# Loading the last residual pair in two column halves, and queueing the stores after the first of them

## The chip, the cores and the metric

The kernel runs on one core of a Trainium2 chip. The metric is the time of one execution in microseconds (us), taken on the device. The profile is one further execution with the hardware profiler; its span runs from the first to the last instruction and is 1.8 us shorter than the time (121.2 us for 123.01 in the profiled run of the kernel before).

## The reference

A 3 x 3 convolution with padding 1 over 16 images of 64 channels and 64 x 64 pixels, 64 channels out, plus a residual:

```python
for b in range(batch):
    for co in range(c_out):
        for ci in range(c_in):
            for kh in range(k):
                for kw in range(k):
                    output[b, co] += weight[co, ci, kh, kw] * x_pad[b, ci, kh:kh+h, kw:kw+w]
return (output + residual).astype(np.float32)
```

Input, residual and output are float32, 16.8 MB each. So 50.48 MB (with the weights) have to move, whatever the kernel does.

## The kernel before

Two images form a pair, on 128 partitions. The residual is loaded into one large tile `ro`, the adds write their result into the same tile, and the stores read it. All loads but one, and all stores, are issued by the sync engine, in one queue. I call each of the 16 DMA engines' part of a queue its ring. It is worked off in order of issue: the store issued at 58.71 us lands at 91.1 us, after the load issued just before it, which lands at 81.3 us.

```python
EARLY = (slice(0, 2), slice(2, 4), slice(4, 6), slice(6, 7))
RES = (slice(0, 1), slice(1, 2), slice(2, 4), slice(4, 6), slice(6, 8))
...
def load_ro(i, e):
    if i >= 2:
        e.wait_ge(s_r[i % 2], 16 * (i // 2))
    return e.dma_start(out=ro[:, RES[i], :], in_=res_bc[:, RES[i], :]).then_inc(s_r[i % 2], 16)
...
for p in range(NPAIR):                      # the sync queue: all loads ...
    if p >= NXR:
        nc.sync.wait_ge(s_half, 2 * (p - NXR) + 3)
    ...
        load_x(p)
    if p in (1, 3, 5, 7):
        load_ro((p + 1) // 2, nc.sync)
for pairs in EARLY:                         # ... and then the stores
    nc.sync.wait_ge(s_add, 2 * pairs.stop + 1)
    store(pairs).then_inc(s_out, 16)
```

The last pair is stored in two column halves at the very end. The scalar engine casts and packs the input, the tensor engine convolves, the vector engine adds the residual (32 adds).

Of the kernel before, what the change touches and what calls it, by code (L numbers as in the profile page):

```python
# [15 lines left out]
def kernel(  # L16
# [7 lines left out]
    nc = tc.nc  # L24
# [6 lines left out]
    NPIX = H * W  # L31
    NPAIR = B // 2
# [4 lines left out]
    NXP = 4  # L37
    NZERO = 4 + 2 * NXP
    EARLY = (slice(0, 2), slice(2, 4), slice(4, 6), slice(6, 7))
    RES = (slice(0, 1), slice(1, 2), slice(2, 4), slice(4, 6), slice(6, 8))  # L40

    res_bc = residual.rearrange("(p b) c h w -> (b c) p (h w)", b=2)
    out_bc = out.rearrange("(p b) c h w -> (b c) p (h w)", b=2)
# [7 lines left out]
    ro = pool.tile([128, NPAIR, NPIX], FP32)  # L51
# [7 lines left out]
    sem = lambda name: tc.alloc_semaphore(name)  # L59
    s_w = sem("s_w")  # L60
    s_x = [sem(f"s_x{i}") for i in range(NXR)]
    s_r = [sem(f"s_r{i}") for i in range(2)]
    s_out = sem("s_out")
    s_id = sem("s_id")
    s_half = sem("s_half")
# [5 lines left out]
    def load_x(p):  # L71
        return nc.sync.dma_start(out=xr[p % NXR][:, :], in_=x_bc[128 * p : 128 * p + 128, :]).then_inc(s_x[p % NXR], 16)

    def load_ro(i, e):
        if i >= 2:
            e.wait_ge(s_r[i % 2], 16 * (i // 2))
        return e.dma_start(out=ro[:, RES[i], :], in_=res_bc[:, RES[i], :]).then_inc(s_r[i % 2], 16)

    def store(pairs, cols=slice(0, NPIX)):
        return nc.sync.dma_start(out=out_bc[:, pairs, cols], in_=ro[:, pairs, cols])  # L80
# [21 lines left out]
    def to_the_front(dma):  # L102



        def fixed(ap):
            t = ap.bass_ap.tensor.name
            return mybir.PhysicalAccessPattern(
                ap=ap.ap, offset=ap.bass_ap.offset, dtype=ap.dtype, memref=t, memsetref=t + "_set", bass_ap=ap.bass_ap
            )  # L110

        front = nc.main_func.blocks[0].instructions
        here = nc.cur_bb.bb.instructions
        ins = here.pop()
        assert ins.name == dma.ins.name
        at = next(
            i for i, e in enumerate(front) if e.engine == ins.engine and isinstance(e, mybir.InstDrain)
        )
        front.insert(at, copy.replace(ins, ins=[fixed(a) for a in ins.ins], outs=[fixed(a) for a in ins.outs]))
# [5 lines left out]
    def weight_block(h, half, d, par, kh):  # L125

        at = 64 * half + 32 * h
        return dict(out=wl[at : at + 32, d, :, par, :], in_=tp[0:32, kh, 0:384].rearrange("p (kw co h) -> p kw co h", kw=3, h=2)[:, :, :, h])

    with tc.tile_critical(no_gpsimd_drain=True):  # L130

        for p in range(NPAIR):
            if p >= NXR:

                nc.sync.wait_ge(s_half, 2 * (p - NXR) + 3)
            if p == 0:
                to_the_front(load_x(p))
                nc.sync.dma_start(out=wraw[:, :], in_=w_rows[:, :]).then_inc(s_w, 16)
            else:
                load_x(p)  # L140
            if p in (1, 3, 5, 7):
                load_ro((p + 1) // 2, nc.sync)
        for pairs in EARLY:
            nc.sync.wait_ge(s_add, 2 * pairs.stop + 1)
            store(pairs).then_inc(s_out, 16)


        nc.gpsimd.memset(ident[:, :], 0.0).then_inc(s_id, 1)  # L148
        nc.gpsimd.wait_ge(s_id, 1)
        nc.gpsimd.affine_select(  # L150
            out=ident[:, :],
            in_=ident[:, :],
            compare_op=mybir.AluOpType.not_equal,
            fill=1.0,
            base=0,
            pattern=[[-1, 128]],
            channel_multiplier=1,
        ).then_inc(s_id, 1)
        nc.gpsimd.wait_ge(s_id, 2)
        for t in xp:  # L160
            nc.gpsimd.memset(t[0:64, 0, :], 0.0).then_inc(s_id, 1)  # L161
            nc.gpsimd.memset(t[64:128, J, :], 0.0).then_inc(s_id, 1)  # L162
        nc.gpsimd.memset(wl[0:64, 0, :, 1, :], 0.0).then_inc(s_id, 1)  # L163
        nc.gpsimd.memset(wl[64:128, 1, :, 0, :], 0.0).then_inc(s_id, 1)  # L164


        to_the_front(load_ro(0, nc.scalar))
        for n in range(B):
            p, im = divmod(n, 2)
            hp = slice(64 * im, 64 * im + 64)  # L170
            x4 = xr[p % NXR].rearrange("q (j two w) -> q j two w", two=2, w=W)
            t = xp[n % NXP]
            if im == 0:
                nc.scalar.wait_ge(s_x[p % NXR], 16 * (p // NXR + 1))
            i = nc.scalar.copy(out=t[64:128, 0:J, :], in_=x4[hp, :, 0, :])  # L175
            i.then_inc(s_half, 1)
            if n >= NXP:
                i._wait_ge(s_conv, n - NXP + 1)
            nc.scalar.copy(out=t[0:64, 1 : J + 1, :], in_=x4[hp, :, 1, :]).then_inc(s_pack, 1)  # L179
            if n == 0:  # L180
                nc.scalar.wait_ge(s_id, NZERO + 1)
                for b in blocks[4:]:
                    for h in range(2):
                        i = nc.scalar.copy(**weight_block(h, *b))  # L184
                i.then_inc(s_id, 1)


        nc.vector.wait_ge(s_id, NZERO + 1)
        for k, b in enumerate(blocks[:4]):
            for h in range(2):  # L190
                i = nc.vector.tensor_copy(**weight_block(h, *b))  # L191
                if k == h == 0:
                    i.then_inc(s_bank, 2)
        i.then_inc(s_id, 1)
        for n in range(B):
            p, im = divmod(n, 2)
            hp = slice(64 * im, 64 * im + 64)
            o4 = ro[:, p, :].rearrange("q (j two w) -> q j two w", two=2, w=W)
            psj = ps[n % 2].rearrange("q c j w -> q (c j) w")
            if im == 0:  # L200
                i = next(i for i, pairs in enumerate(RES) if p < pairs.stop)
                nc.vector.wait_ge(s_r[i % 2], 16 * (i // 2 + 1))
            for par in range(2):
                i = nc.vector.tensor_tensor(  # L204
                    out=o4[hp, :, par, :], in0=psj[64 * par : 64 * par + 64, :, :], in1=o4[hp, :, par, :], op=ADD
                )
                if par == 0:
                    i._wait_ge(s_conv, n + 1)

                i.then_inc(s_add if par == 0 or n == B - 1 else s_bank, 1)  # L210


        nc.tensor.wait_ge(s_id, NZERO)
        nc.tensor.wait_ge(s_w, 16)
        wraw3 = wraw.rearrange("p (ci t) -> p ci t", t=9)
        for t in range(9):
            i = nc.tensor.transpose(  # L217
                out=tp[0:32, t // 3, 128 * (t % 3) : 128 * (t % 3) + 128], in_=wraw3[:, :, t], identity=ident[:, :]
            )
        i.then_inc(s_id, 1)  # L220
        nc.tensor.wait_ge(s_id, NZERO + 3)
        with nc.Fori(0, B // NXP, 1, engines=[PE]):
            for n in range(NXP):
                nc.tensor.wait_ge(s_bank, 1).then_inc(s_bank, -1)
                nc.tensor.wait_ge(s_pack, 1).then_inc(s_pack, -1)  # L225
                order = [(1, 0), (1, 1), (0, 0), (0, 1), (2, 0), (2, 1)]
                for i, (kw, d) in enumerate(order):
                    xlo, xhi = max(0, 1 - kw), min(W, W + 1 - kw)
                    for c in range(NCHUNK):
                        j0 = JC * c  # L230
                        m = matmul(
                            ps[n % 2][:, c, :, xlo:xhi],
                            wl[:, d, kw, :, :].rearrange("q r c -> q (r c)"),
                            xp[n][:, j0 + d : j0 + d + JC, xlo + kw - 1 : xhi + kw - 1],
                            i == 0,
                            i == len(order) - 1,
                            c == 0,
                        )
                m.then_inc(s_conv, 1)


    for h in range(2):
        store(slice(NPAIR - 1, NPAIR), slice(NPIX // 2 * h, NPIX // 2 * (h + 1)))
    with tc.tile_critical(sync_engine=mybir.EngineType.Pool, no_gpsimd_drain=True):
        nc.gpsimd.wait_ge(s_out, 16 * len(EARLY))
        tc.free_semaphores([s_w, *s_x, *s_r, s_out, s_id, s_half, s_pack, s_bank, s_conv, s_add])
# [30 lines left out]
```

## Time and profile before

| | before |
|---|---|
| time, median | 122.92 us (122.90 to 122.94) |
| span of the profile | 121.2 us |
| bytes moved, mean rate over the span | 50.48 MB, 416 GB/s |
| rate in a full stretch | 433 GB/s |
| tensor / vector / scalar engine busy | 86.5 / 76.0 / 63.1 us |
| landing of the last load, of the last store | 81.3 us, 120.3 us |

How to read it: the rate in the full stretches against the mean says that the transfers are the bound, and the difference to the span says how little there is to win. The prediction shows the lines.

Besides the page I use the trace's records of single DMA packets: one row of a transfer, its start, duration and size. In steady traffic a packet of 16 KB takes 611 ns and one of 8 KB takes 309 ns, in nearly every record to the nanosecond; the usual one of 12 KB takes 460 ns, of 4 KB 159 ns. I call **the loss** of a stretch the sum of what its packets took beyond that, divided by 16 engines; gaps in which an engine has no packet are counted apart.

### The profile page before, as it was taken

The numbers are of one execution on the slowest core, as the hardware profiler recorded it, in microseconds if no ns is written. First come the engines' busy times: TensorE is split into PE (matmuls) and PEld (weight loads), VectorE is DVE, ScalarE is ACT, GpSimd is POOL, SyncE is SP. The second block draws the span as 40 slices with busy tenths as digits, with TensorE's granted clock in tenths as the row PEclk, the third lists the DMA queues.
The fourth block names the chain that finished last, engine by engine and source line by source line (L and its number), as shares of the span: only waits on it lengthen the run. The fifth ranks groups of instructions, "written<-read, shape, count | busy, mean of one in ns | idle before, by whom it ended". The sixth has DMA issues, their size and how long they took to land.

```text
span 121.2 us, 735 instructions
## 1 busy us (share of the span) xinstructions
PE 86.5 (71%) x393; PEld 10.6 (9%) x105; DVE 76.0 (63%) x40; ACT 63.1 (52%) x37; POOL 2.4 (2%) x16
## 2 busy tenths in 40 slices
PE   0000609999999999999999999999999998000000
PEld 0000300010101010101010101010101010000000
DVE  0000180088989889898988989889898988930000
ACT  4001999999999755995785958659200000000000
POOL 5200000000000000000000000000000000000000
PEclk9999999999999999999999999999999999955555
DMA  7999999999999999999999999999999999999994
GB/s 232 416 427 438 433 433 433 427 433 433 433 427 433 427 433 433 433 433 433 433 433 433 433 422 427 384 378 433 433 427 427 433 427 433 433 427 433 416 430 181
DMA packets 3648, 50.48 MB, mean 416 GB/s; under 512 B 320, under 2 KB 448, under 8 KB 448
## 3 DMA queue, kind: packets, MB, share of 16 engines
q1 hardware_dynamic: 3504, 48.38, 94.3%
q10 hardware_dynamic: 144, 2.10, 4.1%
HBM read 33.70 MB, written 16.78 MB: 416 GB/s over the span
## 4 chain that ended last, share of the span: by engine, by line
PE 70%; DVEq 2%; DVE 2%; issue 0%
PE ps L87 52%; PE ps L86 18%; DVEq L130 2%; DVE ro L204 2%
## 5 line engine op out<-in xcount | busy, mean ns | idle before, releaser
L204 DVE TENSOR_TENSOR ro<-ps,ro 64x2048 f32<-64x2048 f32 x32 | 73.2, 2289 | 16.3 <-PE ps L87 15.8
L87 PE MATMUL ps<-xp,wl 128*128 128x504 bf16 (+1 forms) x288 | 78.9, 383 | 0.0
L175 ACT CAST xp<-xr 64x2048 bf16<-64x2048 f32 x16 | 30.3, 1896 | 21.1 <-DMA xr<-in_x_dram 11.7
L86 PE MATMUL ps<-xp,wl 128*128 128x504 bf16 (+1 forms) x96 | 36.9, 384 | 3.4 <-PEq L225 3.4
L179 ACT CAST xp<-xr 64x2048 bf16<-64x2048 f32 x16 | 30.4, 1897 | 0.4
L86 PEld LDWEIGHTS ps<-xp,wl 128*128 128x128 bf16 x96 | 9.4, 98 | 77.8 <-issue 77.8
L191 DVE CAST wl<-ps 32x192 bf16<-32x192 f32 x8 | 2.8, 348 | 14.9 <-PE ps L217 14.8
L217 PE MATMUL ps<-ident,wraw 128*32 128x128 f32 x9 | 2.1, 413 | 12.6 <-DMA wraw<-in_weight_dram 12.6
L217 PEld LDWEIGHTS ps<-ident,wraw 128*32 128x32 f32 x9 | 1.2, 137 | 13.1 <-issue 12.6
L175 ACT ACT_TABLE_LOAD x1 | 1.3, 1283 | 1.1 <-SPq L130 1.1
L184 ACT CAST wl<-ps 32x192 bf16<-32x192 f32 x4 | 1.2, 306 | 0.0
L162 POOL MEMSET xp<- 64x64 bf16 x4 | 0.6, 147 | 0.2
L161 POOL MEMSET xp<- 64x64 bf16 x4 | 0.6, 145 | 0.2
L150 POOL TENSOR_SCALAR_AFFINE_SELECT ident<-ident 128x128 f32<-128x128 f32 x1 | 0.3, 295 | 0.2 <-POOL ident L148 0.2
L164 POOL MEMSET wl<- 64x192 bf16 x1 | 0.3, 253 | 0.1
L163 POOL MEMSET wl<- 64x192 bf16 x1 | 0.3, 252 | 0.1
L148 POOL MEMSET ident<- 128x128 f32 x1 | 0.2, 205 | 0.7 <-SPq L130 0.7
L261 POOL MEMSET const-bfloat16-1.0<- 128x1 bf16 x1 | 0.1, 112 | 0.0
L261 POOL MEMSET const-uint8-127<- 128x1 uint8 x1 | 0.1, 112 | 0.0
L261 POOL MEMSET const-float32-1.0<- 128x1 f32 x1 | 0.1, 109 | 0.0
L261 POOL MEMSET const-float32-0.0<- 128x1 f32 x1 | 0.1, 104 | 0.2 <-issue 0.2
## 6 DMA issues: line engine op xcount, KB each, us to landing
xr<-in_x_dram SPq DMA_DIRECT2D x8, 2048.0 KB, 14.8
ro<-in_residual_dram SPq DMA_DIRECT2D x3, 4096.0 KB, 23.1
out_dram<-ro SPq DMA_DIRECT2D x3, 4096.0 KB, 32.2
ro<-in_residual_dram ACTq DMA_DIRECT2D x1, 2048.0 KB, 12.1
ro<-in_residual_dram SPq DMA_DIRECT2D x1, 2048.0 KB, 20.2
out_dram<-ro SPq DMA_DIRECT2D x1, 2048.0 KB, 15.7
out_dram<-ro SPq DMA_DIRECT2D x2, 1024.0 KB, 11.4
wraw<-in_weight_dram SPq DMA_DIRECT2D x1, 144.0 KB, 11.4
```

Source lines behind the costliest of these rows:

```text
L86: return e.matmul(out=out_, lhsT=lhsT, rhs=rhs, start=start, stop=stop, skip_group_check=True)
L87: return e.add_instruction(mybir.InstMatmult(name=nc.get_next_instruction_name(), engine=PE, ins=[e.lower_ap(rhs), e.lower_ap(lhsT)], outs ...
L130: with tc.tile_critical(no_gpsimd_drain=True):
L161: nc.gpsimd.memset(t[0:64, 0, :], 0.0).then_inc(s_id, 1)
L162: nc.gpsimd.memset(t[64:128, J, :], 0.0).then_inc(s_id, 1)
L175: i = nc.scalar.copy(out=t[64:128, 0:J, :], in_=x4[hp, :, 0, :])
L179: nc.scalar.copy(out=t[0:64, 1 : J + 1, :], in_=x4[hp, :, 1, :]).then_inc(s_pack, 1)
L184: i = nc.scalar.copy(**weight_block(h, *b))
L191: i = nc.vector.tensor_copy(**weight_block(h, *b))
L204: i = nc.vector.tensor_tensor(out=o4[hp, :, par, :], in0=psj[64 * par : 64 * par + 64, :, :], in1=o4[hp, :, par, :], op=ADD)
L217: i = nc.tensor.transpose(out=tp[0:32, t // 3, 128 * (t % 3) : 128 * (t % 3) + 128], in_=wraw3[:, :, t], identity=ident[:, :])
L261: nc = _bacc.Bacc("TRN2", target_bir_lowering=False, num_devices=1)
```

## The change

Its intent: stores that queue up behind the last loads are to be kept out of the rings until the loads are nearly through, and yet to come early enough that the rings don't run dry. So the last residual load is cut, and its last megabyte covers the time that issuing the stores takes.

```diff
-    RES = (slice(0, 1), slice(1, 2), slice(2, 4), slice(4, 6), slice(6, 8))
+    WHOLE, LEFT, RIGHT = slice(0, NPIX), slice(0, NPIX // 2), slice(NPIX // 2, NPIX)
+    RES = (
+        (slice(0, 1), WHOLE, None),
+        (slice(1, 2), WHOLE, 1),
+        (slice(2, 4), WHOLE, 3),
+        (slice(4, 6), WHOLE, 5),
+        (slice(6, 7), WHOLE, 7),
+        (slice(7, 8), LEFT, 7),
+        (slice(7, 8), RIGHT, 7),
+    )
+    NR = 3
...
-    s_r = [sem(f"s_r{i}") for i in range(2)]
+    s_r = [sem(f"s_r{i}") for i in range(NR)]
...
-            if p in (1, 3, 5, 7):
-                load_ro((p + 1) // 2, nc.sync)
+            for i, (_, _, behind) in enumerate(RES):
+                if behind == p:
+                    load_ro(i, nc.sync)
+
+        wait_ro(nc.sync, len(RES) - 2)
         for pairs in EARLY:
             nc.sync.wait_ge(s_add, 2 * pairs.stop + 1)
             store(pairs).then_inc(s_out, 16)
```

The vector engine waits for every load that holds a part of its pair, and `load_ro` waits modulo three (cut here).

More of the change, by code (lines that the diff above doesn't have):

```diff
@@ L74, in load_ro, with wait_ro @@
     def load_ro(i, e):
-        if i >= 2:
-            e.wait_ge(s_r[i % 2], 16 * (i // 2))
-        return e.dma_start(out=ro[:, RES[i], :], in_=res_bc[:, RES[i], :]).then_inc(s_r[i % 2], 16)
+        pairs, cols, _ = RES[i]
+        if i >= NR:
+            e.wait_ge(s_r[i % NR], 16 * (i // NR))
+        return e.dma_start(out=ro[:, pairs, cols], in_=res_bc[:, pairs, cols]).then_inc(s_r[i % NR], 16)
+    def wait_ro(e, i):
+        e.wait_ge(s_r[i % NR], 16 * (i // NR + 1))
     def store(pairs, cols=slice(0, NPIX)):
@@ L200 @@
             if im == 0:
-                i = next(i for i, pairs in enumerate(RES) if p < pairs.stop)
-                nc.vector.wait_ge(s_r[i % 2], 16 * (i // 2 + 1))
+                for i, (pairs, cols, _) in enumerate(RES):
+                    if pairs.start <= p < pairs.stop:
+                        wait_ro(nc.vector, i)
             for par in range(2):
@@ L239 @@
                 m.then_inc(s_conv, 1)
-    for h in range(2):
-        store(slice(NPAIR - 1, NPAIR), slice(NPIX // 2 * h, NPIX // 2 * (h + 1)))
+    for cols in (LEFT, RIGHT):
+        store(slice(NPAIR - 1, NPAIR), cols)
     with tc.tile_critical(sync_engine=mybir.EngineType.Pool, no_gpsimd_drain=True):
```

## The prediction

> **What bounds the kernel now.** I read the page first, in the order slices, queues, chain; then the table by stretches of the span; then the sync queue's own waits and its timeline. The slices of the page, the traffic line and the chain come first.
>
> ```profile
> DMA  7999999999999999999999999999999999999994
> GB/s 232 416 427 438 433 433 433 427 433 433 433 427 433 427 433 433 433 433 433 433 433 433 433 422 427 384 378 433 433 427 427 433 427 433 433 427 433 416 430 181
> ...
> HBM read 33.70 MB, written 16.78 MB: 416 GB/s over the span
> ## 4 chain that ended last, share of the span: by engine, by line
> PE 70%; DVEq 2%; DVE 2%; issue 0%
> ```
>
> The first two rows cut the span of 121.2 us into 40 slices of 3.03 us. The DMA row stands at 9 in every slice but the first and the last, and the rate stands at about 433 GB/s. The chain of waits names the tensor engine for 70%, but it adds up to only 74% of the span: it ends with the last add, and what follows, the stores that nobody waits for but the end of the program, isn't in it. So the chain misleads. The traffic decides: 33.70 + 16.78 = 50.48 MB, and 50.48 MB / 0.433 MB per us = 116.6 us. Of the span of 121.2 us only 121.2 - 116.6 = 4.6 us are not transfer at full rate. Any gain must come out of these 4.6 us.
>
> Where they are, the table by stretches shows. Its columns are: stretch, length, busy time of PE, PEld, DVE, ACT and POOL with the number of instructions, granted clock, DMA share, GB/s.
>
> ```profile
> 0.00:1.00 1.00, 0.00 (x0) 0.00 (x0) 0.00 (x0) 0.00 (x0) 0.21 (x4) 1.00 0.00 0
> 1.00:3.50 2.50, 0.00 (x0) 0.00 (x0) 0.00 (x0) 1.28 (x1) 1.67 (x10) 1.00 1.00 334
> ...
> 70.00:77.00 7.00, 7.00 (x34) 0.78 (x8) 5.81 (x4) 4.24 (x4) 0.00 (x0) 1.00 1.02 438
> 77.00:80.50 3.50, 3.50 (x18) 0.39 (x4) 3.47 (x2) 3.48 (x2) 0.00 (x0) 1.00 0.96 323
> 80.50:90.00 9.50, 9.50 (x46) 1.07 (x11) 8.28 (x5) 3.79 (x2) 0.00 (x0) 1.00 1.01 435
> ...
> 119.50:121.20 1.70, 0.00 (x0) 0.00 (x0) 0.00 (x0) 0.00 (x0) 0.00 (x0) 0.50 0.04 14
> ```
>
> Four losses: 1.0 us before the first byte; 2.5 x (433 - 334) / 433 = 0.57 us while the first packets come; 3.5 x (433 - 323) / 433 = 0.89 us between 77.0 and 80.5; and about 1.6 us after the last byte. The third is the only hole within the run, and it is the one which this change is about. The trace's packet records show it more sharply. On each of the 16 engines a packet of 16 KB takes 611 ns, one after the other, from 2 us to 115 us. In between there is one exception: the packets that start between 78 and 79 us take 1092 ns on average, up to 1359 ns. Followed along each engine from 76.5 to 82.5 us, the packets lose 0.71 us against their cadence (mean of 16 engines, 0.43 to 1.03). The last residual load was issued at 58.23 us and took 23.1 us, so it lands at 81.3 us. The hole therefore lies on the last few load packets of every engine, just before the ring turns from loads to stores. It looks like a cost of this turn.
>
> **Who queues what, and when.** The sync queue issues all loads and then the stores:
>
> ```profile
> 58.23 0.43 SPq L77 DMA_DIRECT2D ro<-in_residual_dram  x1
> 58.71 0.47 SPq L80 DMA_DIRECT2D out_dram<-ro  x1
> ```
>
> The first store follows the last load by 0.48 us, because the adds that it waits for are long done (the 32 adds start at 24.8 us, in pairs 5.19 us apart; pairs 0 and 1 are complete at about 47.8 us). It then lies behind some 20 us of loads, and its 32.4 us to landing are nearly all queueing. The later stores are released by adds:
>
> ```profile
> SPq L80 <- DVE ro L204: 39.8, 3, 20.3
> ```
>
> With the adds' cadence, the releases come at 24.8 + 8 x 5.19 + 2.3 = 68.6 us for pairs 2 and 3, at 89.4 us for pairs 4 and 5 (the timeline shows 89.37), at 99.8 us for pair 6, and 107.5 us for the last two halves. The data of the last store before those ends at about 115 us. So from 58 us on there are always at least 7 us of work in the rings, and compute is off the path by that much.
>
> **What the Trainium skill says.** "DMA: Bandwidth & Descriptors", section "Where 436 GB/s comes from", gives 435 GB/s as the ceiling of 16 ports; the trace agrees, with 433 to 438 GB/s in the full stretches, so a steady stretch can't be improved. The same page, "Queues, rings and completion order", says that an engine takes descriptors of one ring in ring order and that each completion count is a strongly ordered write. That agrees: the store issued at 58.71 lands at 91.1 us, and its own 4.19 MB / 0.433 = 9.7 us of data follow on the load's landing at 81.3 us. The same page, "Latency and other measured facts", gives about 600 ns to the first byte for a transfer issued on the sync queue. Here the first transfer, issued at 0.00, has its first packet at 1.02 us; I use 1.02. No page names a cost for turning one ring from loads to stores.
>
> **The change part by part.**
>
> 1. Three semaphores for the residual in place of two. The waits before issuing move: pairs 4 and 5 wait for pair 0, pair 6 for pair 1, the left half of pair 7 for pairs 2 and 3 (landed at 22.7 + 19.0 = 41.7 us), the right half for pairs 4 and 5, issued at 38.07 and landed 23.1 us later, at 61.2 us. The right half is thus issued at about 61.2 us in place of 58.23. About 17 us of loads are still in the rings then. Cost: 0.
>
> 2. One load of 4 MB becomes one of 2 MB and two of 1 MB, the latter with rows of 8 KB. Two more issues of 0.43 us on a queue with slack. The packets of 8 KB are as good: the final stores have them too, at 309 ns each, 2 x 309 = 618 against 611 ns, and there are 16 of them per engine, so 16 x 3.5 ns = 0.06 us. The vector engine needs pair 6 at 24.8 + 12 x 5.19 = 87.1 us and pair 7 at 97.5 us, both long after 81 us. Cost: below 0.1 us.
>
> 3. All stores wait for the left half. It lands one megabyte before the end of the loads, at 1.05 / 0.433 = 2.42 us before: about 78 us. Stores one and two (their adds done at 47.8 and 68.6 us) are then issued back to back; store three waits for 89.4 us as before. The rings must not run dry in between. The sum: the count is complete only when the slowest engine is, and the 16 counts of the last residual load came in over 0.54 us (trace, landing records); the count follows the last data by about 0.35 us (the completion packet at 80.47, landing at 80.80 us on the first engine); then 1.02 us from issue to first packet. 0.54 + 0.35 + 1.02 = 1.91 us of 2.42 us. So there are some 0.5 us left on the fastest engine: no gap, but not by much.
>
> 4. What it may win: the hole. If it comes from stores queued behind loads (an engine reading ahead into them while its last loads are in flight), then it shrinks, since nothing is behind those loads until the last 1 to 1.5 us. Then up to 0.71 us go. If it is the cost of the turn itself, it only moves to the last packets of the right half, and nothing is won.
>
> 5. After the turn both kernels write 16.78 MB in 39 us without a break. A shift at the turn carries through to the end one to one, since the last stores have 7 us of slack.
>
> **The rivals.** *The hole goes.* For it: the hole lies on loads that have stores behind them, and no other boundary between two loads has it; it begins about 2.4 us before the loads would end without it, a right half's worth. Against: the start of the run shows packets of 1.0 to 1.5 us as well, with no store in sight, so long packets may belong to any new kind of traffic. Time: 122.92 - 0.71 = 122.2 us. *The hole stays, the issue is hidden.* For it: the same number of turns, in the same ring. Time: 122.9 us. *The hole stays and the rings run dry.* For it: the slack of 0.5 us is of the size of the skew of the engines, and a delay to first byte of 1.6 us would use it up; the start also has 0.57 us of slow first packets. Time: 122.92 + 0.2 to 0.7 us, say 123.4. *The stores collide with compute.* Against: compute has 7 us of slack. I give it nothing.
>
> **Range and chances.** I give the first 0.35, the second 0.4, the third 0.25: 0.35 x 122.2 + 0.4 x 122.9 + 0.25 x 123.4 = 122.8 us. The range is from the hole gone with a little besides, 122.0 us, to the hole doubled or a gap of 0.6 us, 123.5 us. Two per cent is 2.46 us. To win that, more than half of the 4.6 us that aren't full-rate transfer would have to go, and three of its four parts aren't touched; to lose it, the rings would have to stand still for 2.5 us, that is a landing-to-first-packet time of 4.4 us where 1.9 are expected. Faster 0.01, same 0.97, slower 0.02.
>
> **What would show it.** In the profile of the changed kernel, the timeline of the sync queue should have the first store at 78 to 79 us, and the second right behind it. In the stretches, the hole between 77 and 81 us decides: 430 GB/s throughout means the first rival, a hole of 0.7 to 0.9 us the second, a stretch with a DMA share well below 0.9 and zero packets the third. Store three should still be issued near 89.4 us, and the adds should keep their 5.19 us. The prediction is wrong if the first store is issued past 80 us, if adds wait for a residual load, or if rate or order of the loads before 75 us change.

## The result, and the profile after

The changed kernel took 122.34 us (median of 4, 122.23 to 122.36), the kernel before on the same chip 122.91 us (122.89 to 122.94). The ratio is 0.9952 with a 95% interval of 0.9935 to 0.9969. Ratios here are the mean time of one kernel's runs over the mean of the other's in the same rounds, so not quite the ratio of the medians. It is faster by half a per cent: "same" by the 2% rule, but clear of noise.

The slices of the changed kernel's page, for the two rows that the prediction showed of the kernel before:

```profile
DMA  7999999999999999999999999999999999999994
GB/s 239 413 435 430 430 430 430 430 435 430 430 424 424 435 430 435 424 435 435 430 435 435 435 435 402 432 454 430 435 430 430 430 424 435 419 430 430 421 427 185
...
HBM read 33.70 MB, written 16.78 MB: 419 GB/s over the span
```

The two slices of 384 and 378 GB/s are gone. A single slice of 402 is left, beside one of 454: packets are counted where they fall, and slices of 3 us hold few of them. The table by stretches says it more plainly, for the stretches that the prediction showed (stretch, length, busy time of the five engines, granted clock, DMA share, GB/s):

```profile
1.00:3.50 2.50, 0.00 (x0) 0.00 (x0) 0.00 (x0) 1.28 (x1) 1.67 (x11) 1.00 0.99 341
...
70.00:77.00 7.00, 6.95 (x33) 0.78 (x8) 5.82 (x4) 4.24 (x4) 0.00 (x0) 1.00 1.00 425
77.00:80.50 3.50, 3.50 (x18) 0.39 (x4) 3.47 (x2) 3.48 (x2) 0.00 (x0) 1.00 1.03 438
80.50:90.00 9.50, 9.50 (x46) 1.07 (x11) 8.28 (x5) 3.90 (x3) 0.00 (x0) 1.00 1.02 436
```

Between 77.0 and 80.5 us the rate is 438 GB/s in place of 323. (The 425 GB/s from 70 to 77 us, where the kernel before had 438, are no loss: the packet records have none there, and the run with the cut alone shows 424.) In the packet records the loss between 77 and 81 us is 0.71 us before and 0 after; no engine has a gap there either, in either kernel. The last landing moves from 120.3 to 119.6 us, by the same 0.7 us, and the span from 121.2 to 120.5 us.

The sync queue's timeline, and what it waited for, in the changed kernel:

```profile
58.34 3.07 SPq L88 DMA_DIRECT2D ro<-in_residual_dram  x3
78.14 31.09 SPq L94 DMA_DIRECT2D out_dram<-ro  x6
```

```profile
SPq L94 <- DVE ro L222: 20.4, 2, 10.4
SPq L94 <- DMA ro<-in_residual_dram: 16.6, 1, 16.6
```

The first store is issued at 78.14 us in place of 58.71, the second 0.44 us after it; store three still goes at 89.47 us. The queue spends 16.6 us waiting for the left half, and half as long as before for adds (20.4 in place of 39.8 us). Both are idle times of a queue that is not the bottleneck, and cost nothing. The busy times of the tensor, vector and scalar engine are those of before: 86.5, 76.0 and 63.1 us, and the adds still take 2289 ns each.

### The profile page after: what moved, and what is told of

The parts are those of the page before. It is cut to its first block, busy times and chain, and to the rows that moved or that the text cites. A ratio compares the mean times of both kernels' runs of the same rounds, so it can differ in the third digit from the quotient of the medians. Undisturbed runs are those within 1.5% of the kernel's fastest.

```text
span 120.5 us, 734 instructions
## 1 busy us (share of the span) xinstructions
PE 86.5 (72%) x389; PEld 10.7 (9%) x105; DVE 76.0 (63%) x40; ACT 63.1 (52%) x37; POOL 2.4 (2%) x16
## 4 chain that ended last, share of the span: by engine, by line
PE 70%; DVEq 2%; DVE 2%; issue 0%
PE ps L101 53%; PE ps L100 17%; DVEq L144 2%; DVE ro L222 2%
## 5 line engine op out<-in xcount | busy, mean ns | idle before, releaser
L222 DVE TENSOR_TENSOR ro<-ps,ro 64x2048 f32<-64x2048 f32 x32 | 73.2, 2289 | 16.5 <-PE ps L101 16.0
L101 PE MATMUL ps<-xp,wl 128*128 128x504 bf16 (+1 forms) x288 | 79.1, 384 | 0.2
L100 PE MATMUL ps<-xp,wl 128*128 128x504 bf16 (+1 forms) x92 | 35.4, 385 | 3.4 <-PEq L243 3.4
## 6 DMA issues: line engine op xcount, KB each, us to landing
out_dram<-ro SPq DMA_DIRECT2D x3, 4096.0 KB, 20.4
```

Source lines behind the costliest of these rows:

```text
L100: return e.matmul(out=out_, lhsT=lhsT, rhs=rhs, start=start, stop=stop, skip_group_check=True)
L101: return e.add_instruction(mybir.InstMatmult(name=nc.get_next_instruction_name(), engine=PE, ins=[e.lower_ap(rhs), e.lower_ap(lhsT)], outs ...
L222: i = nc.vector.tensor_tensor(out=o4[hp, :, par, :], in0=psj[64 * par : 64 * par + 64, :, :], in1=o4[hp, :, par, :], op=ADD)
```

## The experiments

The change does two things, the cut and the wait. My theory at this point: stores lying in the ring behind the last loads make the hole, so the wait does it, and the cut only makes the wait possible. The rivals: the cut (8 KB packets, three semaphores) does it, or the hole grows with how long or how much is queued. Every experiment has one profile, and each was timed in five rounds against the kernel before, whose median in the four groups, each on a chip of its own, was 122.97, 122.92, 122.91 and 122.89 us.

### The changed kernel again

> The changed kernel as it stands, as a control on the same chip as the others. 122.3 us, 0.995 of the kernel before; no hole between 77 and 81 us.

Measured: 122.43 us, ratio 0.9959 (0.9946 to 0.9972), no loss between 77 and 81 us. The gain holds on another run.

### The cut without the wait

```diff
-        wait_ro(nc.sync, len(RES) - 2)
         for pairs in EARLY:
```

> The changed kernel without the wait of the stores for the left half: the last pair still in two halves, three semaphores, but the first store queued at some 61 us behind 17 us of loads. Theory (stores lying in the ring behind the last loads make the hole): the hole of 0.7 us is back, 122.9 us. Rival (the halves, or their 8 KB packets, or the semaphores make the difference): no hole, 122.3 us.

Measured: 123.06 us, ratio 1.0007 (0.9995 to 1.0019). Stretch from 77.0 to 80.5 us:

```profile
77.00:80.50 3.50, 3.50 (x18) 0.39 (x4) 3.47 (x2) 3.48 (x2) 0.00 (x0) 1.00 1.02 365
```

The hole is back, with a loss of 0.56 us, and the whole gain is gone. Halves, small packets and a third semaphore win nothing by themselves.

### The wait without the cut, at 9.7 us before the end of the loads

```diff
+        nc.sync.wait_ge(s_x[7 % NXR], 16 * (7 // NXR + 1))
         for pairs in EARLY:
```

> The kernel before with one wait added: the stores are queued when the last input load has landed, that is about 9.7 us before the loads end, in place of 20 us; the last residual load stays one of 4 MB with rows of 16 KB. Theory (an engine reads ahead into the stores over its last few packets, so what counts is whether a store is in the ring some 2.5 us before the end): the hole of 0.7 us stays, 122.9 us. Rival (the hole grows with how long or how many stores lie queued): half of it goes, 122.6 us.

Measured: 122.96 us, ratio 1.0001 (0.9989 to 1.0013); first store issued at 70.96 us, 337 GB/s from 77.0 to 80.5 us, loss 0.66 us. The stores waited for 12 us less than before and the hole is as large. So it doesn't grow with the time in the ring.

### The last pair whole, stores 4.8 us before the end

```diff
-        (slice(7, 8), LEFT, 7),
-        (slice(7, 8), RIGHT, 7),
+        (slice(7, 8), WHOLE, 7),
```

> The changed kernel with the last pair loaded whole (2 MB, rows of 16 KB) and the stores queued when pair 6 has landed: about 4.8 us before the loads end, so that the first store reaches the ring some 3.3 us before. Theory of reading ahead by about 2.5 us: most of the hole is back, 122.7 to 122.9 us, on packets that start after the store came. Rival (any wait of this kind that avoids a long queue helps, the halves are not needed): no hole, 122.3 us.

Measured: 122.95 us, ratio 0.9999 (0.9987 to 1.0011); first store issued at 75.83 us.

```profile
77.00:80.50 3.50, 3.50 (x18) 0.39 (x4) 3.46 (x2) 3.47 (x2) 0.00 (x0) 1.00 0.96 323
```

The whole hole, loss 0.74 us, with the same 323 GB/s as in the kernel before. So two megabytes of loads behind the wait are too many.

### Three quarters behind the wait

```diff
-        (slice(7, 8), LEFT, 7),
-        (slice(7, 8), RIGHT, 7),
+        (slice(7, 8), slice(0, 1024), 7),
+        (slice(7, 8), slice(1024, 4096), 7),
```

> The changed kernel with the last pair loaded as one quarter and three quarters, the stores waiting for the quarter: 1.5 MB, 3.6 us, of loads are left, so that the first store reaches the rings about 2.2 us before the loads end (with the half 1.0 us, no hole; with the whole pair 3.3 us, the whole hole). Theory of reading ahead over the last 2.5 us or so: by then most of the reads of the last loads are done, so a part of the hole at most, 122.3 to 122.7 us. If the hole is whole, 122.9 us, the reach of what makes it is shorter than 2.2 us.

Measured: 122.71 us (122.47 to 123.11), ratio 0.9983 (0.9967 to 0.9998); first store issued at 77.45 us.

```profile
77.00:80.50 3.50, 3.50 (x18) 0.39 (x4) 3.47 (x2) 3.48 (x2) 0.00 (x0) 1.00 1.02 434
```

The loss there is 0.02 us: there is no hole. But between 75 and 77 us, before the first store was issued, packets lost 0.27 us, nearly all of it on those of 4 KB: they took 190 ns on average where the usual one took 159. So the run gave away a part of what the wait won. The equal halves of the changed kernel have no such loss; why the uneven pieces have it is not shown. Judged by the hole at the turn, its edge lies between this run and the one before: a first store issued at 75.83 us has all of it, one issued at 77.45 us none. The loads end between 80 and 81 us.

### One quarter behind the wait

```diff
-        (slice(7, 8), LEFT, 7),
-        (slice(7, 8), RIGHT, 7),
+        (slice(7, 8), slice(0, 3072), 7),
+        (slice(7, 8), slice(3072, 4096), 7),
```

> The changed kernel with the last pair loaded as three quarters and one quarter, the stores waiting for the three quarters: 0.5 MB, 1.2 us, of loads are left to cover the issue in place of 2.4. By my sum of 1.9 us for the fastest engine and 1.4 us for the slowest the rings run dry for 0.2 to 0.7 us: 122.6 to 122.9 us, and packets of stores that start after a gap. If the rings stay full, the issue costs less than I summed, and the time is 122.3 us.

Measured: 122.92 us, ratio 1.0000 (0.9987 to 1.0013). The profiled execution, at 123.38 us, was the slowest of the five.

```profile
77.00:80.50 3.50, 3.50 (x18) 0.39 (x4) 2.89 (x3) 2.51 (x2) 0.00 (x0) 1.00 0.85 323
```

Compare this with the line of the whole pair above: the same 323 GB/s, but a DMA share of 0.85 in place of 0.96. There the engines were busy with packets that took too long; here, at the end of the stretch, they had no packets. The store was issued at 80.03 us, and its first packets start between 80.95 and 81.10 us, on all 16 engines, after gaps of 0.63 us on average. From issue to first packet are 0.92 to 1.07 us, and the sum in the prediction was right: a quarter is too short a cover. These first store packets take some 608 ns, as any other. A first store that met empty engines was not slow.

The equal 323 GB/s are partly chance, for this run has slow packets too: between 76 and 79 us its packets of 12 KB lost 0.33 us (501 ns on average, the usual one takes 460), all before any store was issued. Gaps and loss make 0.96 us, close to the 1.04 us by which this execution lies above the median of the changed kernel; the other four executions (122.90 to 122.98 us) have no profile. So load packets can be slow without any store, here as in the three quarters; the record doesn't show why.

### One store early, the others after the wait

```diff
+    EARLY = (slice(0, 1), slice(1, 2), slice(2, 4), slice(4, 6), slice(6, 7))
...
-        wait_ro(nc.sync, len(RES) - 2)
-        for pairs in EARLY:
+        for k, pairs in enumerate(EARLY):
+            if k == 1:
+                wait_ro(nc.sync, len(RES) - 2)
```

> The changed kernel, but the store of pair 0 alone (2 MB) is queued at once, at about 61 us; the others wait for the left half as in the change. Theory (one store behind the loads is enough): the whole hole of 0.7 us is back, 122.9 to 123.0 us. Rival (the hole grows with the amount that is queued): a quarter of it, 122.5 us.

Measured: 122.93 us, ratio 1.0000 (0.9988 to 1.0013).

```profile
77.00:80.50 3.50, 3.50 (x18) 0.48 (x5) 3.10 (x2) 3.10 (x2) 0.00 (x0) 1.00 1.02 377
```

The loss is 0.43 us. A quarter of the queued bytes makes more than half of the hole in the profile and takes the whole gain in time. One store is enough.

### Two turns from loads to stores

To double the suspected cost, the store of pair 0 goes ahead of the last input load, in the kernel before:

```diff
+    EARLY = (slice(0, 1), slice(1, 2), slice(2, 4), slice(4, 6), slice(6, 7))
...
+            if p == 7:
+                nc.sync.wait_ge(s_add, 3)
+                store(EARLY[0]).then_inc(s_out, 16)
...
-        for pairs in EARLY:
+        for pairs in EARLY[1:]:
```

> The kernel before with the store of pair 0 (2 MB) moved ahead of the last input load in the sync queue, so that the ring turns from loads to stores twice, once near 70 us and once near 85 us, and from stores to loads once. Theory (each turn with stores queued behind loads costs some 0.7 us, on the load packets just ahead of the turn): two holes, the first about 2.5 us ahead of the first store packet, and 123.6 us. Rival (the hole belongs to the end of the loading, or to a time near 78 us): one hole, 122.9 us.

Measured: 123.26 us, ratio 1.0021 (1.0008 to 1.0034). Stretches around the first turn, at 66 us, and the second, at 85.5 us:

```profile
63.00:66.00 3.00, 3.00 (x15) 0.39 (x4) 2.97 (x2) 2.51 (x2) 0.00 (x0) 1.00 0.96 284
66.00:70.00 4.00, 4.00 (x21) 0.44 (x5) 3.39 (x3) 2.81 (x2) 0.00 (x0) 1.00 1.03 442
83.00:86.00 3.00, 3.00 (x16) 0.31 (x4) 2.97 (x2) 2.98 (x2) 0.00 (x0) 1.00 1.03 437
```

Here my theory fell. The first turn has a hole, a larger one (loss 0.90 us), so the hole belongs neither to a time near 78 us nor to the end of the loading. But the second turn, with stores that had lain behind the loads for more than 20 us, has next to none (0.03 us). And the turn back from stores to loads costs nothing. The hole is not the price of every turn.

### Two turns far apart

The first turn might have left too few loads behind it for a second hole. So the same store goes two input loads earlier (`if p == 5:` in place of `if p == 7:`).

> Like two_turns, but the store of pair 0 stands ahead of the sixth input load, so that the first turn from loads to stores is near 45 us and the second near 85 us, with 14 MB of loads between them in place of 6 MB. In two_turns the first turn had a hole of 0.9 us and the second none. Theory A (the first large store of a run has the hole, later turns do not): one hole, near 43 to 45 us, 123.2 us. Theory B (a long unbroken run of loads builds up what makes the hole, and 6 MB were too few): two holes, 123.7 us. Theory C (the hole belongs to a time near 78 us or to the last loads): one hole at the second turn; two_turns speaks against it.

Measured: 123.42 us, ratio 1.0043 (1.0031 to 1.0055).

```profile
40.00:43.00 3.00, 3.00 (x16) 0.29 (x3) 2.42 (x2) 2.01 (x2) 0.00 (x0) 1.00 1.00 426
43.00:46.00 3.00, 3.00 (x16) 0.39 (x4) 2.54 (x2) 1.78 (x1) 0.00 (x0) 1.00 1.01 284
...
83.00:86.00 3.00, 3.00 (x16) 0.39 (x4) 2.97 (x2) 2.95 (x3) 0.00 (x0) 1.00 1.00 426
```

One hole again, at the first turn (loss 1.04 us between 43 and 46 us), and no loss at the second, 40 us and 14 MB of loads later. This is theory A of the expectation: the first large store of an execution has the hole. The time is some 0.2 us more than A said. The first hole is 0.33 us larger here than that of the kernel before, which would cover this; why it is larger I don't know.

### The first store in the other ring

```diff
+            if n == 9:
+                nc.scalar.wait_ge(s_add, 3)
+                nc.scalar.dma_start(out=out_bc[:, EARLY[0], :], in_=ro[:, EARLY[0], :]).then_inc(s_out, 16)
```

(with `EARLY` cut as above, and the other stores after the left half.)

> The changed kernel with the store of pair 0 alone issued early, at about 58 us, from the scalar queue, that is in the other ring of each engine, so that its packets run between packets of loads; the other stores wait for the left half. Theory (what hurts is a store behind the last loads in the same ring): no hole at 77 to 80 us, and 122.3 to 122.5 us if loads and stores side by side run at full rate. Rival (any meeting of loads and stores in an engine costs): a lower rate while both run, near 58 to 68 us, and 122.9 us or more.

Measured: 123.08 us, ratio 1.0011 (0.9999 to 1.0024). The scalar queue issued the store at 51.09 us, earlier than I had put it.

```profile
51.09 0.36 ACTq L199 DMA_DIRECT2D out_dram<-ro  x1
...
53.00:56.00 3.00, 3.00 (x15) 0.33 (x4) 2.66 (x2) 1.90 (x1) 0.00 (x0) 1.00 1.03 350
56.00:60.00 4.00, 4.00 (x21) 0.44 (x5) 3.70 (x2) 3.71 (x2) 0.00 (x0) 1.00 1.00 422
...
82.00:85.00 3.00, 3.00 (x16) 0.39 (x4) 2.65 (x2) 2.97 (x2) 0.00 (x0) 1.00 1.03 437
```

The hole follows the first store: it now lies at 53 us, two microseconds after that store was issued (loss 0.72 us from 53 to 57 us), and the turn, now at about 85.5 us, has none. In the packet records every slow packet of this hole is one of a load, started between 53.1 and 56.4 us, while the store's own first packet starts only at 55.50 us, 4.4 us after its issue, and takes the usual 611 ns. So it is the loads that are held up, and 0.66 of the 0.72 us fall on packets that start before the store's first. Then loads and stores run side by side until the store lands at 66.6 us, at 422 GB/s and more: their meeting in an engine costs nothing in itself. So the position behind loads in the same ring, which I had taken for the cause, isn't needed for the hole. The rival of this expectation, a lower rate for as long as both run, fell too, although the time is in the range that it named: one hole of the usual size, in another place, accounts for a time like that of the kernel before.

### Using up the first store with a tiny one

If the first store of an execution pays, a tiny one might pay for it. Twice in the kernel before, with a piece of the output that the last store overwrites (each followed by a wait for its landing before the large stores):

```diff
+            if p == 2:                       # first variant: behind the third input load
+                nc.sync.wait_ge(s_id, 2)
+                nc.sync.dma_start(out=out_bc[:, 7, 0:128], in_=ident[:, :]).then_inc(s_out, 16)
```

```diff
+        to_the_front(nc.scalar.dma_start(    # second variant: the first transfer on the scalar queue
+            out=out_bc[:, 7, 0:128], in_=res_bc[:, 7, 0:128]).then_inc(s_out, 16))
         to_the_front(load_ro(0, nc.scalar))
```

> The kernel before with one tiny store (64 KB of the identity tile into a place of the output that the last store overwrites later) in the same sync ring behind the third input load, about 20 us into the run; the large stores are queued early as before. In two_turns the second turn had no hole. Theory (only the first store of a run makes a hole, whatever its size, by stopping the loads that are being read when its turn comes near): the hole of about 0.7 us moves to some 2.5 us ahead of the tiny store, near 20 us, and the turn at 80 us has none; 122.9 to 123.1 us, the 64 KB being 0.15 us of traffic. Rival (the hole belongs to a turn of all 16 engines at once from loads to a long run of stores): the hole stays at 77 to 80 us; 123.1 us, or 123.8 with a hole at both.

Measured: 123.06 us, ratio 1.0011 (0.9998 to 1.0024). The tiny store passes at 26 us in packets of 512 B of 27 ns each, and the 16 KB packets before and after it take their 611 ns: no hole there. At the large turn 370 GB/s remain, a loss of 0.52 us. The tiny store doesn't use the cost up.

> The kernel before with a tiny write to the output (64 KB copied within HBM, to the same place, overwritten later) as the very first transfer on the scalar queue, at 0 us; the large stores are queued early as before. Theory of the first store: whatever it costs lies in the first 2 us, where packets are slow anyway, and the turn at 80 us has no hole: 122.2 to 122.6 us, a gain without waiting for the left half. Rival (the cost belongs to the turn, or to the first store of this very ring): the hole of 0.7 us stays at 77 to 80 us, 123.0 us.

Measured: 123.08 us, ratio 1.0021 (1.0004 to 1.0039).

```profile
77.00:80.50 3.50, 3.50 (x18) 0.39 (x4) 3.47 (x2) 2.71 (x2) 0.00 (x0) 1.00 0.99 407
```

Here the turn at 80 us keeps 407 GB/s and has a loss of only 0.13 us, but the packets of the first 3 us lose 0.99 us in place of 0.54. The start lost about what the turn gained, and nothing is won. That the one is the other, moved, is not shown: the extra copy also changed the traffic at the start. The two tiny stores differ in source (the tile, or HBM), ring and time, so they don't tell what uses the cost up.

## Why the prediction was right

The time, 122.34 us, lies in the range of 122.0 to 123.5 us, and "same" at 2% was right. That alone says little, since all three outcomes lay in the range; the outcome that I thought likeliest, the hole that stays, did not come. By its steps:

- **The bound.** Right. Nothing but the DMA traffic moved the time: what was lost or won in the rings near 50, 66 or 80 us came out at the end, while the vector engine's busy time stayed at 76.0 us in every run and the scalar engine's at 63.1 to 63.2 (the tensor engine's lay between 86.5 and 88.0, without a link to the time).
- **Parts 1 and 2, semaphores and halves: no cost, no gain.** Right; the cut without the wait is 1.0007. The right half was held back for the landing of pairs 4 and 5 (the queue's waits show 1.8 us in `load_ro`, once) and nothing came of it. The halves run at full rate; only the uneven quarters didn't.
- **Part 3, the cover.** Right. Expected were 78 to 79 us for the first store, measured is 78.14. The spread of the counts was 0.37 us (77.75 to 78.12 us) in place of 0.54. With 0.92 to 1.07 us from issue to first packet, the store reached the engines near 79.1 to 79.2 us; the right half ran out at 79.77 us on the first engine. So 0.6 us were to spare where I had summed 0.5. The quarter shows what lies beyond: gaps of 0.63 us. One sum was off without moving anything: for rings that stand still for 2.5 us, the time from landing to first packet would have to be 2.42 + 2.5 = 4.9 us, not 4.4.
- **Part 4, the hole.** Its size was right: 0.71 us predicted as the most that could go, 0.71 us went in the trace, and 0.57 us in the medians. My weights were off: I gave 0.35 to its going and 0.4 to its staying, so the point of 122.8 us is 0.46 us above the result. The argument for staying, "the same number of turns, in the same ring", counted turns as the cause; the two kernels with two turns show that a second turn has no hole.
- **The reason for the hole.** I wrote "If it comes from stores queued behind loads (an engine reading ahead into them while its last loads are in flight)". The first half is only half right. Stores behind loads are where it showed; what the runs show is narrower. The first large store of an execution (2 or 4 MB here) delays the load packets in flight as it comes near by 0.4 to 1.0 us per engine, in either of the two rings tried, and later ones don't (the run with the tiny copy at the start is the exception, with 0.13 us). It made no hole when at most some 3 us of loads were left at its issue (issued at 77.45 us or later, for loads that end between 80 and 81), nor when it met empty engines. The change wins by placing the first store there.

The runs side by side, with the place and size of the hole from the packet records:

| kernel | first large store issued, us | hole, loss per engine | time, us |
|---|---|---|---|
| before | 58.7 | 77 to 80 us, 0.71 us | 122.91 |
| changed | 78.1 | none | 122.34 |
| cut without the wait | 61.5 | 78 to 80 us, 0.56 us | 123.06 |
| wait without the cut | 71.0 | 77 to 80 us, 0.66 us | 122.96 |
| three quarters behind the wait | 77.5 | none at the turn (0.27 us before the store, 75 to 77 us) | 122.71 |
| one quarter | 80.0 | none at the turn, but gaps of 0.63 us (and 0.33 us before the store, 76 to 79 us) | 122.92 |
| whole pair | 75.8 | 77 to 80 us, 0.74 us | 122.95 |
| one store early | 61.6 | 78 to 80 us, 0.43 us | 122.93 |
| two turns | 48.9 | 63 to 66 us, 0.90 us; second turn 0.03 us | 123.26 |
| two turns apart | 38.1 | 43 to 46 us, 1.04 us; second turn 0 | 123.42 |
| other ring | 51.1 | 53 to 57 us, 0.72 us; turn 0 | 123.08 |
| tiny store from the tile first | 59.1 | 78 to 81 us, 0.52 us | 123.06 |
| tiny copy at the start | 58.0 | 78 to 80 us, 0.13 us; start 0.99 in place of 0.54 us | 123.08 |

**What stays open.** What the engine does in that microsecond is not shown: the records tell how long packets took, not why. Reading ahead is a guess that fits the edge between 75.83 and 77.45 us; it doesn't say why it happens once. Nor is it settled why a tiny store from a tile leaves most of the hole and a tiny copy at the start leaves little, nor why the hole is 0.71 us in one kernel and 1.04 in another: with one profile each, differences of 0.2 us between holes prove nothing. The prediction's remark that long packets may belong to any new kind of traffic was not tested either: the first loads lose 0.4 to 0.6 us in every run but one, with no store near, and the first large store has about as much; and the slow load packets of the two uneven cuts, before any store, fit neither. No experiment beat the changed kernel.

## What to carry to other kernels

In a kernel bound by transfers, divide bytes by the full rate, and look for the holes in the rate over short stretches; a hole with a high DMA share is slow packets, one with a low share is empty rings, and the cures are opposite. Stores that are ready early needn't be queued early: of the cuts tried here the best was to issue the first of them when about one megabyte of loads was left, enough to cover the microsecond from issue to first packet, and late enough that the loads showed no hole. And before a cost is put down to "every turn", double the turns: here the second was free.

## What the Trainium skill lacked or had wrong

- No page has it that the first large store of an execution can hold up the loads in flight. The runs with the large store as the first show a loss of 0.43 to 1.04 us per engine, once (0.71 us in the kernel before), and 0.00 to 0.03 us at a second turn from loads to stores. It would belong to "DMA: Bandwidth & Descriptors", "Latency and other measured facts".
- "DMA: Bandwidth & Descriptors", "Latency and other measured facts", gives some 600 ns to the first byte of a transfer from the sync queue. Here the start of the DMA instruction and the first packet are 1.02 us apart for the first load and 0.92 to 1.07 us for a store that met empty engines. The DMA instruction itself takes 0.39 us at the first load and 0.40 us at that store, so counted from its end it is 0.63 and 0.52 to 0.67 us, and the page's figure holds. The page doesn't say from where it counts; a cover that is sized from the start of the instruction needs the larger figure. A first packet can also come much later: 4.4 us after the issue for the store from the scalar queue, beside running loads.
- The same page, "Issuing engines are not separate DMA queues", says that transfers from different engines interleave on the same 16 DMA engines. The run with a store from the scalar queue agrees for a store among loads: 422 GB/s or more while both ran, after one hole of 0.72 us, which the page doesn't mention.
